# Split weights kept in DRAM after the first block, and chains issued by an estimate of the engines' queues

## The chip, the cores and the metric

The kernel runs on one core of a Trainium2 chip. The time is the device time of one execution in microseconds; the runs of one kernel are summarised by their median.

## What is computed

One layer of a hybrid decoder for 2048 prompt tokens (after 16 learned meta tokens) and 8 sample sequences of 4 tokens, in float32, model width 1024. Four heads of width 128 are retention heads, four are gated delta heads; then come an output projection, a residual LayerNorm, a SwiGLU FFN of width 2816 and another LayerNorm. The core of it, from the reference:

```python
proj = h @ w_in                                     # both head groups, 1024 -> 4104
# retention, chunks of 128 tokens
scores = jnp.einsum('bnhid,bnhjd->bnhij', q, k) * decay
intra = jnp.einsum('bnhij,bnhjd->bnhid', scores, v)
s = chunk_decay * s + jnp.einsum('bhcd,bhce->bhde', kc, vc)
# gated delta rule, chunks of 128 tokens
kk = jnp.einsum('bnhid,bnhjd->bnhij', k, k)
lower = jnp.where(strict, kk * decay, 0.0) * beta[..., :, None]
a_mat = jnp.eye(C, dtype=q.dtype) + lower
sol = lax.linalg.triangular_solve(a_mat, rhs, left_side=True, lower=True, unit_diagonal=True)
u = wv - jnp.einsum('bhcd,bhde->bhce', wk, s)
o = jnp.einsum('bhcd,bhde->bhce', qg, s) + jnp.einsum('bhij,bhje->bhie', at, u)
s = cd * s + jnp.einsum('bhcd,bhce->bhde', kt, u)
# both
mixed = jnp.concatenate([o_r, o_g], -1) @ w_out
hp = layer_norm(ALPHA * hp + mp, ln1_g, ln1_b)
hp = layer_norm(ALPHA * hp + swiglu(hp, w_gate_up, w_down), ln2_g, ln2_b)
```

## The kernel before

**Products in two parts.** A float32 product is made of three matmuls on float32r parts: a value `x` is split into `xh`, its cast, and `xl = x - xh`, and `mm3` (L288) issues `ah bh`, `ah bl` and `al bh`. Weights come from DRAM in float32 and are split on the chip each time they are used: for a piece of 2048 columns, `load_piece` issues two DMAs of 512 KB into the ring `raw` of two buffers (L260, on SyncE's queue, SP), and `split` casts each on ScalarE (ACT, `wh<-raw`, L237) and subtracts on VectorE (DVE, `wl<-raw,wh`, L244). The pair goes to `wring`, which has two buffers: the piece in use and the one after it. `next_piece` hands over the piece whose turn it is and starts the load of the next; with `later=True` the split is put on the list `pend` and issued a few steps later.

**Attention.** The tokens are taken in four blocks of 512 (block 0 holds 48 more rows, meta and sample tokens). In each block the eight heads come in the order "r0 g0 r1 g1 r2 g2 r3 g3" (the last block has another), and each takes two pieces of weights, so the same 16 pieces are loaded and split in each of the four blocks, 64 in all. The projections of a head (`ret_proj`, `gdn_proj`) are long runs of matmuls into the PSUM pool `pj` that depend on little. What follows for a head is a chain of small products, each of which waits for other engines: `ret_chain` for retention; `gdn_chain` with `gdn_group` for the delta rule. The latter makes `LT` from `kT` (L816, L818), then `Z` and `U` on DVE (L827, L828) and the six masks `Lm` on GpSimd (POOL, L830), inverts by block doubling (L834 reads U; L840 and L847 make the products of each level), refines the inverse (the tile `Tf`, L860, L868), runs the recurrence over four chunks (L902 to L922), scales the output on DVE (`V<-V,rqy`, L931) after a reciprocal square root in small DVE steps (`rqa`, `rqt`, `rqy`, L189 to L201), and transposes it (L933).

**The weaving.** The chains are Python generators. While the projections of the next head are issued, `mm3g` yields after every six matmuls or so the time that these take on TensorE (PE), and `advance` subtracts it from a counter for each chain; when the counter is used up, the next step of the chain is issued. What a step puts into its counter is a number of the list `LAT`, which is fixed by hand per kind of step, times 1.0 for retention and 1.8 for the delta rule (`SLACK`). So a step's distance from the one before is a fixed amount of projection work. One retention chain and one delta chain can be under way at a time. Every engine runs its instructions in the order that results from this.

**FFN.** After the attention phase the output projection and the FFN run over two halves of the tokens in the same manner (L1067 on). They are not touched.

Of the kernel before, what the change touches and what calls it, by code (L numbers as in the profile page):

```python
# [148 lines left out]
class _Cut:  # L149
    """Allocates [128, full, ...] tiles and hands out their first n rows of dim 1."""  # L150
# [13 lines left out]

class Builder:
    def __init__(self, tc, I, O):
        self.tc, self.nc, self.I, self.O = tc, tc.nc, I, O
        _, self.off, self.gam, _ = _consts()
        self.es = ExitStack()
# [13 lines left out]
    def rsqrt(self, x, n, rows, pool, scale, eps):  # L183
        """(scale x + eps)^-0.5; x may be a list of equal parts."""
# [19 lines left out]
    def layer_norm(self, src, rows, g, b, pool, fast=False, pinned=False):  # L204
        """LayerNorm of rows in place; src is the row, or its two halves. fast: the vector engine alone."""
# [42 lines left out]
    def load_piece(self, src, ab=False, ring=None, later=False, el="dve"):  # L248
        """2048 (+64) columns of weights as a pair of float32r parts."""
# [7 lines left out]
        lv = l.rearrange("p (a b) -> p a b", a=8)  # L257
        for i in range(2):
# [17 lines left out]
    def mm3g(self, out, lh, ll, rh, rl, kn, per):  # L276
        """As mm3, with a yield of the tensor engine's time after every few k."""
# [6 lines left out]
    def mm3(self, out, lh, ll, rh, rl, kn, first=True, last=True):  # L284
        """out (+)= sum_k l(k)^T r(k), with float32 operands in two float32r parts."""
# [55 lines left out]
    def phase_ln(self, b):  # L341
        """Embedding LayerNorm of the tokens of block b, a tile at a time."""
# [11 lines left out]
    def first_block(self):  # L354
        """As phase_ln and turned for the first block, whose tokens and weights are loaded together."""
# [14 lines left out]
        self.ahead = self.load_piece(*self.todo.pop(0), el="pool")  # L370
# [23 lines left out]
    def phase_t(self, b, tiles, x=None):  # L394
        """Transposes of normalised rows, one tile of tokens at a time."""
# [14 lines left out]
    def next_piece(self):  # L410
        """The weights whose turn it is; the load of those after them starts."""
        w = self.ahead
        while self.pend:
            self.split(*self.pend.pop(0))
        self.age = 0
        self.ahead = self.load_piece(*self.todo.pop(0), later=True) if self.todo else None
        return w

    def ret_proj(self, b, h, gates, out, before=None):
# [39 lines left out]
        if before and b == 0:  # L459
            # the weights come before the tokens: each tile of these meets all of those  # L460
# [20 lines left out]
    def ret_chain(self, b, h, qkvg, mixd):  # L481
        """The retention itself; yields the time until its next products can start."""
# [62 lines left out]

        flip(0)
        yield LAT[0]
        for t in range(n):
            score(t)
            yield LAT[1]  # L550
            if t + 1 < n:
                flip(t + 1)
                yield LAT[2]
            mix(t)
            yield LAT[3]
        rs = self.rsqrt(ss[:, :n], n, 128, self.sm, 4.0 / HD, 4.0 * RMS_EPS)
        yield LAT[4]
        for t, (rows, c0, ch) in enumerate(tiles):
            orow = NS if ch < 0 else 128
            o = oc[t]  # L560
            nc.vector.scalar_tensor_tensor(out=o, in0=o, scalar=rs[:orow, t:t + 1], in1=vg[t][1][:orow], op0=ALU.mult, op1=ALU.mult)
            p = self.prt.tile([128, 128], F32, tag="rt", name="rt")[:, :orow]
# [5 lines left out]
            yield LAT[5]  # L568
# [3 lines left out]
    def state_out(self, kt, u, S0, cd, gam, out):  # L572
        """out_b = decay_b S0_b + kt_b^T u_b for the eight sample sequences."""
# [367 lines left out]
    def attention(self):  # L941
        with ExitStack() as es:
# [21 lines left out]
            while self.active:  # L964
                self.advance(0.3)
# [23 lines left out]
    def finish(self, key):  # L989
        while key in self.active:  # L990
            self.advance(0.3)
# [258 lines left out]
```

## Time and profile before

| | us |
|---|---|
| three runs | 3137.73, 3143.98, 3137.69 |
| median | 3137.73 |
| the profiled execution: its span | 3141.4 |
| PE busy | 2994.8 |
| DVE busy | 1826.4 |
| ACT busy | 967.1 |
| POOL busy | 565.9 |

No time of its own is given for the profiled execution beside its span; the span lies between the shortest and the longest of the three runs, 3.7 above the median. Busy times are sums over the whole span. The attention phase ends at about 1362 us; its blocks begin at about 0, 396, 721 and 1028 us. The trace's rows name a line of the kernel, an engine, an operation and the tiles "out<-in"; PE's times of matmuls are modelled at their ends, so that neighbouring rows overlap.

### The profile page before, as it was taken

The numbers are of one execution on the slowest core, as the hardware profiler recorded it, in microseconds if no ns is written. First come the engines' busy times: TensorE is split into PE (matmuls) and PEld (weight loads), VectorE is DVE, ScalarE is ACT, GpSimd is POOL, SyncE is SP. The second block draws the span as 40 slices with busy tenths as digits, with TensorE's granted clock in tenths as the row PEclk, the third lists the DMA queues.
The fourth block names the chain that finished last, engine by engine and source line by source line (L and its number), as shares of the span: only waits on it lengthen the run. The fifth ranks groups of instructions, "written<-read, shape, count | busy, mean of one in ns | idle before, by whom it ended". The sixth has DMA issues, their size and how long they took to land. (4 is left out here: it accounts for less than half of the span.)

```text
span 3141.4 us, 44842 instructions
## 1 busy us (share of the span) xinstructions
PE 2994.8 (95%) x17858; PEld 2593.6 (83%) x17858; DVE 1826.4 (58%) x4024; ACT 967.1 (31%) x2179; POOL 565.9 (18%) x570
## 2 busy tenths in 40 slices
PE   7999998999999988999999999999999999999997
PEld 6988887888888877878999999998777877878787
DVE  7777777877787777767333333333684343333346
ACT  2434443545544545433111111111233111111111
POOL 1332222221222122202100001110131000001002
PEclk9999998999999999999999999999999999999999
DMA  5222222222222111152111111112242111111111
GB/s 198 85 75 79 95 99 79 88 93 88 78 93 97 59 53 66 48 180 64 54 41 54 41 41 54 41 41 68 71 145 81 41 54 41 54 41 54 40 41 54
DMA packets 91986, 225.28 MB, mean 72 GB/s; under 512 B 10960, under 2 KB 39168, under 8 KB 91776
## 3 DMA queue, kind: packets, MB, share of 16 engines
q1 hardware_dynamic: 91776, 222.41, 21.5%
q8 instruction: 140, 2.29, 0.3%
q14 instruction: 70, 0.57, 0.1%
HBM read 191.87 MB, written 30.51 MB: 71 GB/s over the span
## 5 line engine op out<-in xcount | busy, mean ns | idle before, releaser
L288 PE MATMUL g<-fxT,wh 128*128 128x352 f32 (+2 forms) x3648 | 954.9, 344 | 1.5 <-DVE th L1110 0.6
L288 PEld LDWEIGHTS g<-fxT,wh 128*128 128x128 f32 x3648 | 646.6, 188 | 62.8 <-ACT fxT L237 1.0
L288 PE MATMUL d<-wh,ff 128*128 128x512 f32 (+1 forms) x1912 | 618.3, 397 | 15.8 <-DVE y L1129 6.9
L288 PE MATMUL g<-fxT,wl 128*128 128x352 f32 (+2 forms) x1824 | 626.9, 344 | 0.0
L237 ACT CAST wh<-raw 128x1024 fp32r<-128x1024 f32 x276 | 285.4, 1050 | 637.9 <-PE d L288 407.5
L288 PE MATMUL pj<-wh,xT 128*128 128x256 f32 (+2 forms) x2176 | 458.0, 298 | 14.5 <-DVE rotB L440 8.1
L288 PEld LDWEIGHTS d<-wh,ff 128*128 128x128 f32 (+1 forms) x1912 | 351.1, 184 | 116.5 <-DVE y L1129 16.8
L244 DVE TENSOR_TENSOR wl<-raw,wh 128x1024 fp32r<-128x1024 f32 x274 | 356.5, 1313 | 56.5 <-ACT wh L237 54.8
L288 PE MATMUL pj<-xT,wh 128*128 128x512 f32 (+1 forms) x1280 | 380.3, 379 | 0.8 <-DVE kp L685 0.6
L288 PE MATMUL d<-wl,ff 128*128 128x512 f32 (+1 forms) x956 | 377.9, 395 | 1.7 <-DVE wl L244 1.7
L244 POOL TENSOR_TENSOR ff<-th,ff 128x352 fp32r<-128x352 f32 (+2 forms) x114 | 142.7, 1251 | 1299.7 <-ACT ff L237 1254.8
L288 PEld LDWEIGHTS pj<-wh,xT 128*128 128x128 f32 (+1 forms) x2176 | 357.8, 193 | 20.3 <-issue 8.6
L288 PEld LDWEIGHTS g<-fxT,wl 128*128 128x128 f32 x1824 | 342.4, 188 | 28.8
L1129 DVE TENSOR_TENSOR y<-y,d 128x512 f32<-128x512 f32 (+1 forms) x340 | 231.6, 685 | 187.3 <-PE d L288 187.1
L288 PE MATMUL pj<-wl,xT 128*128 128x256 f32 (+2 forms) x1088 | 319.3, 294 | 0.5 <-POOL wl L244 0.5
L1110 DVE SCALAR_TENSOR_TENSOR th<-th,g 128x352 f32<-128x352 f32 (+2 forms) x114 | 65.2, 572 | 338.3 <-ACT th L1109 338.3
L1111 DVE SCALAR_TENSOR_TENSOR th<-th,g 128x352 f32<-128x352 f32 (+2 forms) x114 | 65.2, 572 | 336.9 <-PE g L288 336.7
L288 PE MATMUL pj<-xT,wl 128*128 128x512 f32 (+1 forms) x640 | 230.1, 360 | 0.0
L288 PEld LDWEIGHTS pj<-xT,wh 128*128 128x128 f32 x1280 | 209.0, 192 | 19.4 <-DVE S L584 3.0
L288 PEld LDWEIGHTS d<-wl,ff 128*128 128x128 f32 (+1 forms) x956 | 175.7, 184 | 44.9 <-DVE wl L244 2.7
L288 PEld LDWEIGHTS pj<-wl,xT 128*128 128x128 f32 (+1 forms) x1088 | 210.4, 193 | 1.1 <-POOL wl L244 0.8
L1109 ACT ACTIVATE th<-g 128x352 f32<-128x352 f32 (+2 forms) x114 | 57.7, 506 | 371.8 <-PE g L288 343.0
(272 smaller groups left out, 3812.6 us busy)
## 6 DMA issues: line engine op xcount, KB each, us to landing
raw<-gu SPq DMA_DIRECT2D x88, 512.0 KB, 3.9
raw<-wret SPq DMA_DIRECT2D x64, 512.0 KB, 4.0
raw<-wgd SPq DMA_DIRECT2D x64, 512.0 KB, 3.9
raw<-dn SPq DMA_DIRECT2D x44, 512.0 KB, 3.9
raw<-wout SPq DMA_DIRECT2D x16, 512.0 KB, 4.2
ff<-mixd SPq DMA_DIRECT2D x16, 512.0 KB, 4.1
y<-xhat SPq DMA_DIRECT2D x16, 512.0 KB, 4.8
out_y<-y SPq DMA_DIRECT2D x16, 512.0 KB, 2.6
```

What stands on the lines that cost most here:

```text
L237: i = nc.scalar.copy(out=h, in_=src)
L244: i = (nc.vector if el == "dve" else nc.gpsimd).tensor_tensor(out=l, in0=src, in1=h.bitcast(F32), op=ALU.subtract)
L288: self.nc.tensor.matmul(out, lhsT=a(k), rhs=b(k), start=first and k == 0 and i == 0, stop=last and k == kn - 1 and i == 2)
L1109: nc.scalar.activation(out=t, in_=ps[0], func=AF.Tanh, scale=0.5)
L1110: nc.vector.scalar_tensor_tensor(out=t, in0=t, scalar=1.0, in1=ps[0], op0=ALU.add, op1=ALU.mult)
L1111: nc.vector.scalar_tensor_tensor(out=t, in0=t, scalar=0.5, in1=ps[1], op0=ALU.mult, op1=ALU.mult)
L1129: nc.vector.tensor_tensor(out=ys, in0=ys, in1=p, op=ALU.add)
```

## The change

**Weights.** Each entry of the list of pieces now has a block and a key. In block 0 a piece is loaded and split as before, and when its turn comes, `next_piece` also writes its two parts to DRAM (the tiles `parts`, 1 MB for `wh` and 1 MB for `wl`). In blocks 1 to 3 `load_piece` reads the two parts back into `wring` with two DMAs and splits nothing.

**Weaving.** `LAT` and `SLACK` are gone. All engine calls go through wrappers that tell a `Meter` of each instruction. It keeps one clock for each engine: an instruction begins when its engine is free and its inputs are made (0.12 us later if another engine made them), and takes a time that is linear in its elements. The PSUM pools are wrapped in `Ring`, which knows when the next buffer comes free. A step of a chain now yields what its next product needs (tiles and pools), and `advance` issues it as soon as the Meter has all of it ready 0.35 us before the end of PE's queue.

```diff
-SLACK = {"r": 1.0, "g": 1.8}
+MARGIN = 0.35
-LAT = [1.0, 0.7, 0.7, 0.7, 2.0, 0.7, 0.5, 1.2, 1.8, 0.9, 1.0, 1.0, 1.7, 1.0, 0.6, 0.5, 0.5]
...
+class Meter:
+    BASE = {"vector": (0.17, 0.00088), "scalar": (0.19, 0.00078), "gpsimd": (0.12, 0.0025)}
+    HOP = 0.12
...
+    def when(self, need):
+        return max([0.0] + [n.next_free() if isinstance(n, Ring) else self.made.get(self.name(n), (0.0, 0))[0] + self.HOP for n in need])
...
+        a, b = self.BASE[engine]
+        if op == "bn_stats":
+            n = 512
+        return a + b * n + (0.2 if kw.get("accum_out") is not None else 0.0)
...
+        t = self.free[engine]
+        for a in ins:
+            end, by = self.made.get(self.name(a), (0.0, engine))
+            t = max(t, end + (0.0 if by == engine else self.HOP))
...
+        end = t + self.took(engine, op, out, kw)
+        self.free[engine] = end
...
+        if kept is not None:
+            for i, t in enumerate((h, l)):
+                nc.sync.dma_start(out=t.bitcast(F32), in_=kept[i, :, :n])
+            return hv, lv
+        if keep is not None:
+            self.keeping[id(hv)] = keep[:, :, :n], h, l
...
+    def load_next(self, **how):
+        b, key, src, ab = self.todo.pop(0)
+        if b == 0:
+            self.parts[key] = self.dr.tile([2, 128, self.wcols], F32, tag=f"parts{key}", name="parts")
+            return self.load_piece(src, ab, keep=self.parts[key], **how)
+        return self.load_piece(src, ab, kept=self.parts[key])
...
     def next_piece(self):
         w = self.ahead
         while self.pend:
             self.split(*self.pend.pop(0))
+        if id(w[0]) in self.keeping:
+            to, *parts = self.keeping.pop(id(w[0]))
+            for i, t in enumerate(parts):
+                self.nc.sync.dma_start(out=to[i], in_=t.bitcast(F32))
         self.age = 0
-        self.ahead = self.load_piece(*self.todo.pop(0), later=True) if self.todo else None
+        self.ahead = self.load_next(later=True) if self.todo else None
...
-        yield LAT[8]
+        yield kT, self.pw
         pl = wide()
...
-        yield LAT[9]
+        yield U, self.pw
         pt = wide()[:R, :m, :R]
...
         for x in range(1, nl):
-            yield LAT[10]
+            yield T, Lm, self.pw
...
+        nc.vector.tensor_tensor(out=O[:orow], in0=O[:orow], in1=rs.unsqueeze(2).broadcast_to([orow, m, 128]), op=ALU.mult)
+        yield O, self.psc
         p = self.psc.tile([128, 4, 128], F32, tag="sc", name="sc")[:, :m, :orow]
-        nc.vector.tensor_tensor(out=O[:orow], in0=O[:orow], in1=rs.unsqueeze(2).broadcast_to([orow, m, 128]), op=ALU.mult)
...
-    def advance(self, us):
+    def advance(self):
         for key in list(self.active):
-            c = self.active[key]
-            c[1] -= us
-            while c[1] <= 0:
-                w = next(c[0], None)
-                if w is None:
+            while key in self.active:
+                c = self.active[key]
+                if self.m.when(c[1]) > self.m.free["tensor"] - MARGIN:
+                    break
+                need = next(c[0], None)
+                if need is None:
                     del self.active[key]
-                    break
-                c[1] += w * SLACK[key]
+                else:
+                    c[1] = need
...
     def finish(self, key):
         while key in self.active:
-            self.advance(0.3)
+            self.advance()
+            if key in self.active:
+                t = min(self.m.when(c[1]) for c in self.active.values()) + MARGIN
+                self.m.free["tensor"] = max(self.m.free["tensor"], t)
```

The two kernels' orders differ at many places. Three are shown. The lists name an instruction's line, operation and tiles; in the changed kernel every instruction has the line of the wrapper, L262, so there the tiles tell them apart.

DVE in block 1, where the third delta head (g2) begins its inverse while the chain of the head before it (tile `V_8073`, in the other kernel `V_7996`) ends. First before, from the last state product on:

```order
L922 SCALAR_TENSOR_TENSOR V_8073<-qs,eg,w 128x128
L244 TENSOR_TENSOR wl<-raw,wh 128x1024
...
L199 TENSOR_TENSOR rqt<-rqy 128x4
L244 TENSOR_TENSOR wl<-raw,wh 128x1024
...
L818 TENSOR_TENSOR LT<-w,mg 128x512
L200 SCALAR_TENSOR_TENSOR rqt<-rqt,rqa 128x4
L827 TENSOR_TENSOR Z<-LT,lvl 128x512
L201 SCALAR_TENSOR_TENSOR rqy<-rqt,rqy 128x4
L439 TENSOR_TENSOR qk<-pj,rott 128x256
L929 TENSOR_TENSOR rqy<-rqy,gsk 128x4
L828 SCALAR_TENSOR_TENSOR U<-Z,ident 128x512
L931 TENSOR_TENSOR V_8073<-V_8073,rqy 128x512
```

The same place after the change:

```order
L262 SCALAR_TENSOR_TENSOR V_7996<-qs,eg,w 128x128
L262 TENSOR_SCALAR rkd<-qk,cb 128x128
L262 TENSOR_TENSOR vb<-w,sv 128x512
...
L262 TENSOR_TENSOR LT<-w,mg 128x512
L262 SCALAR_TENSOR_TENSOR rqy<-rqt,rqy 128x4
L262 TENSOR_TENSOR Z<-LT,lvl 128x512
L262 TENSOR_TENSOR rqt<-rqy 128x4
L262 SCALAR_TENSOR_TENSOR U<-Z,ident 128x512
L262 SCALAR_TENSOR_TENSOR rqt<-rqt,rqa 128x4
L262 TENSOR_TENSOR qk<-pj,rott 128x256
L262 SCALAR_TENSOR_TENSOR rqy<-rqt,rqy 128x4
...
L262 TENSOR_TENSOR V_7996<-V_7996,rqy 128x512
```

The two subtractions behind the last state product are gone, `vb` has moved behind it, and `qk` now comes after U.

PE at the same place, from the product that makes LT's input (`w<-kT`) to the transposes of V (`sc<-ident`); the projection matmuls in between are `pj`, three to a step. Before:

```order
L816 MATMUL w<-kT 128x128 x4
L288 MATMUL pj<-wh,xT 128x256
L288 MATMUL pj<-wl,xT 128x256
L288 MATMUL pj<-wh,xT 128x256 x2
...
L288 MATMUL pj<-wh,xT 128x256 x2
L834 LDWEIGHTS U
L834 MATMUL w<-identh,U 128x128
...
L288 MATMUL pj<-wl,xT 128x256
L288 MATMUL pj<-wh,xT 128x256 x2
L933 MATMUL sc<-ident,V_8073 128x128 x4
```

And after:

```order
L262 MATMUL w<-kT 128x128 x4
L262 MATMUL pj<-wh,xT 128x256 x2
L262 MATMUL pj<-wl,xT 128x256
...
L262 MATMUL pj<-wh,xT 128x256
L262 LDWEIGHTS U
L262 MATMUL w<-identh,U 128x128
...
L262 MATMUL pj<-wh,xT 128x256 x2
L262 MATMUL pj<-wl,xT 128x256
L262 MATMUL pj<-wh,xT 128x256
L262 MATMUL sc<-ident,V_7996 128x128 x4
```

Between `w<-kT` and U stand 25 projection matmuls before and 19 after; between the last state product of the other chain and the transposes of V, 60 before and 37 after.

SP at the start of the kernel, where the second piece of weights is asked for. Before:

```order
L378 DMA xhat<-x 128x512 x2
L260 DMA raw<-wret 128x1024 x2
L524 DMA S_807<-st_ret 128x1024
L378 DMA xhat<-x 128x512 x2
L260 DMA raw<-wgd 128x1024 x2
```

And after:

```order
L262 DMA xhat<-x 128x512 x2
L262 DMA parts<-wh 128x2048
L262 DMA parts<-wl 128x2048
L262 DMA raw<-wret 128x1024 x2
L262 DMA xhat<-x 128x512 x2
L262 DMA S_855<-st_ret 128x1024
L262 DMA parts<-wh 128x2112
L262 DMA parts<-wl 128x2112
L262 DMA raw<-wgd 128x1024 x2
```

The stores of a piece's two parts stand ahead of the loads of the piece after it.

More of the change, by code (lines that the diff above doesn't have):

```diff
@@ new lines, with __init__, next_free, tile @@
+class Ring:
+    of = {}
+    def __init__(self, pool, bufs, meter):
+        self.pool, self.bufs, self.meter = pool, bufs, meter
+        self.busy, self.at = [0.0] * bufs, 0
+    def next_free(self):
+        return self.busy[self.at % self.bufs]
+    def tile(self, *a, **kw):
+        t = self.pool.tile(*a, **kw)
+        i = self.at % self.bufs
+        self.at += 1
+        n = self.meter.name(t)
+        self.meter.used[n] = self.busy[i]
+        Ring.of[n] = self, i
+        return t
+class Timed:
+    def __init__(self, engine, key, meter):
+        self.engine, self.key, self.meter = engine, key, meter
+    def __getattr__(self, op):
+        f = getattr(self.engine, op)
+        def issue(*a, **kw):
+            i = f(*a, **kw)
+            self.meter.note(self.key, op, a, kw)
+            return i
+        return issue
@@ L165, with __init__ @@
+class Engines:
+    def __init__(self, nc, meter):
+        for k in ("tensor", "vector", "scalar", "gpsimd", "sync"):
+            setattr(self, k, Timed(getattr(nc, k), k, meter))
 class Builder:
     def __init__(self, tc, I, O):
-        self.tc, self.nc, self.I, self.O = tc, tc.nc, I, O
+        self.m = Meter()
+        Ring.of = {}
+        self.tc, self.nc, self.I, self.O = tc, Engines(tc.nc, self.m), I, O
         _, self.off, self.gam, _ = _consts()
@@ L246, in split, with load_piece @@
             self.tc.keep_in_program_order(i)
-    def load_piece(self, src, ab=False, ring=None, later=False, el="dve"):
+    def load_piece(self, src, ab=False, ring=None, later=False, el="dve", keep=None, kept=None):
         nc = self.nc
@@ L369, in first_block @@
         g, be = [self.vec_bcast(i, self.ax, "xa") for i in range(2)]
-        self.ahead = self.load_piece(*self.todo.pop(0), el="pool")
+        self.ahead = self.load_next(el="pool")
         load(0, "kT")
@@ L856, in gdn_group @@
         nc.scalar.copy(out=V, in_=U)
-        yield LAT[12]
+        yield T, LT, self.pw
         pe = wide()[:R, :m, :R]
@@ L864, in gdn_group @@
         for it in range(2):
-            yield LAT[13]
+            yield Er, V, self.pw
             pu = wide()[:R, :m, :R]
@@ L950, in attention @@
             self.mp = self.pool("mix", bufs=2, es=es)
-            self.pj = self.pool("p_pj", bufs=2, space=PSUM, es=es)
-            self.pw = self.pool("p_w", bufs=3, space=PSUM, es=es)
-            self.psc = self.pool("p_sc", bufs=1, space=PSUM, es=es)
-            self.prt = self.pool("p_rt", bufs=2, space=PSUM, es=es)
+            self.pj = Ring(self.pool("p_pj", bufs=2, space=PSUM, es=es), 2, self.m)
+            self.pw = Ring(self.pool("p_w", bufs=3, space=PSUM, es=es), 3, self.m)
+            self.psc = Ring(self.pool("p_sc", bufs=1, space=PSUM, es=es), 1, self.m)
+            self.prt = Ring(self.pool("p_rt", bufs=2, space=PSUM, es=es), 2, self.m)
             self.todo, self.pend = [], []
+            self.parts, self.keeping = {}, {}
             for b in range(NBLK):
@@ L963, in attention @@
                 self.attn_block(b)
-            while self.active:
-                self.advance(0.3)
+            for key in ("r", "g"):
+                self.finish(key)
             nc.sync.dma_start(out=self.O["conv"], in_=self.cout)
@@ L1022, in attn_block @@
             for i, us in enumerate(fill):
-                self.advance(us)
+                self.advance()
                 self.age += 1
```

71 lines of the change are left out of this document (56 added, 15 removed).

## The prediction

> **What bounds the kernel now.** I read the page's head and its busy table first, then the windows by stage, then what TensorE (PE) waits for, then what VectorE (DVE) does in a stretch where PE waits.
>
> ```profile
> span 3141.4 us, 44842 instructions
> PE 2994.8 (95%) x17858; PEld 2593.6 (83%) x17858; DVE 1826.4 (58%) x4024; ACT 967.1 (31%) x2179; POOL 565.9 (18%) x570
> ...
> 0.00:40.00 40.00, 20.94 (x117) 18.32 (x118) 32.68 (x96) 9.67 (x15) 7.75 (x15) 0.87 0.73 247
> 40.00:396.00 356.00, 340.99 (x2617) 304.77 (x2615) 264.97 (x707) 154.83 (x466) 99.48 (x118) 0.98 0.28 92
> 396.00:721.00 325.00, 302.42 (x2127) 260.63 (x2127) 250.90 (x640) 154.56 (x412) 77.16 (x87) 0.95 0.27 88
> 721.00:1028.00 307.00, 286.23 (x2073) 252.23 (x2074) 236.85 (x610) 151.05 (x395) 72.46 (x80) 0.97 0.27 88
> 1028.00:1362.00 334.00, 305.07 (x2220) 267.41 (x2219) 251.90 (x605) 157.95 (x412) 75.86 (x90) 0.97 0.18 60
> 1362.00:3141.00 1779.00, 1739.09 (x8711) 1490.26 (x8709) 789.15 (x1372) 339.05 (x480) 233.19 (x180) 0.99 0.18 60
> ```
>
> A window row gives length, busy time of PE, its weight loads, DVE, ACT and POOL, the granted clock, DMA share and GB/s. The rows are the start, attention blocks 0 to 3, and the FFN. PE bounds the span, so time is saved only where PE stands still or runs at a low clock. In blocks 1 to 3, the ones the weight part touches, PE is idle for 22.58 + 20.77 + 28.93 = 72.3 us of 966, and the clock costs another 325 x 0.05 + 307 x 0.03 + 334 x 0.03 = 35.5 us. The FFN loses 40 us of 1779 and its code is unchanged. All that the change could win is therefore some 108 us, 3.4%, and DVE, busy 77% of these blocks on average, is the engine to look at.
>
> ```profile
> PE w L834 <- DVE U L828: 22.8, 12, 3.5
> PE sc L933 <- DVE V L931: 15.4, 11, 3.1
> PE pj L288 <- DVE rotB L440: 7.7, 3, 3.1
> PE sc L910 <- DVE r L905: 5.8, 7, 1.3
> PE pt L406 <- DVE rqy L201: 4.6, 2, 2.3
> ...
> L244 DVE TENSOR_TENSOR wl<-raw,wh 128x1024 fp32r<-128x1024 f32 x96 | 119.8, 1254 | 10.0 <-ACT wh L237 9.6
> ```
>
> These are PE's waits in 396:1362 (total, times, longest) and the largest DVE group there. Nearly every wait ends with DVE. Two of them, U at the start of the delta rule's inverse and V, the scaled output of the previous head's chain, make 38.2 us. One stretch shows how:
>
> ```profile
> 632.00:668.00 36.00, 30.43 (x213) 27.00 (x212) 34.55 (x88) 13.91 (x38) 14.24 (x13) 0.97 0.37 121
> 668.00:715.00 47.00, 47.00 (x339) 41.17 (x337) 29.23 (x61) 26.35 (x64) 4.88 (x10) 0.95 0.28 84
> ...
> 658.25 1.21 DVE L244 TENSOR_TENSOR wl<-raw,wh 128x1024 fp32r<-128x1024 f32 x1
> ...
> 661.49 0.69 DVE L818 TENSOR_TENSOR LT<-w,mg 128x512 f32<-128x512 f32 x1
> ...
> 662.82 1.11 DVE L201 SCALAR_TENSOR_TENSOR rqy<-rqt,rqy 128x4 f32<-128x4 f32 x1
> ...
> 664.97 0.68 DVE L828 SCALAR_TENSOR_TENSOR U<-Z,ident 128x512 f16<-128x512 f16 x1
> 665.57 1.64 DVE L931 TENSOR_TENSOR V<-V,rqy 128x512 f32<-128x512 f32 x1
> ...
> 665.71 0.61 PE L834 MATMUL w<-identh,U 128*128 128x128 f16 x4 [3.48 <-DVE U L828]
> ```
>
> For 36 us DVE is 96% busy and PE is not, and then PE runs without a gap while DVE has slack. So PE does not wait for one slow operation: DVE has fallen behind, and U and V come last in its queue. A single DVE item taken out anywhere in that stretch brings U nearer by its own length. The stretch is the third delta head of block 1, whose rows of the order stand above.
>
> **The weight part.** It takes 96 subtractions of 1.254 us off DVE in blocks 1 to 3 (the row above) and as many casts off ACT, which binds nothing. The 120 us are not the gain: only what lies in a stretch where DVE is behind counts. To size it I went, for each of the twelve delta heads of these blocks, from the last product of the previous chain's inverse (the tile Tf) to this head's U and to the V that follows, and summed along both orders the DVE work and the PE work that lie between, each kind of instruction at its mean duration in the trace. DVE work minus PE work is what PE must wait if DVE never rests.
>
> Before: 6.9 us in each of four heads, 5.9 in two, 3.2, 2.5 and 2.3 in three, 0.2 or less in three. Sum 48. The head quoted is one with 6.9 (38.2 of DVE against 31.3 of PE). Its measured gaps in that stretch are 36.00 - 30.43 = 5.6 us, so the method reads a little high. With the change: 5.6 in four heads, 2.9 in two, none in the others. Sum 28. Four subtractions stood in most of these windows and none does now.
>
> **The weave part** is in that same sum, since the orders of the changed kernel hold both. It works in the opposite direction at these two places. Chains are let go sooner, and the cover becomes thinner: the PE work between the product that makes LT's input and the one that reads U falls from 3.74 to 2.37 us (median of the sixteen heads), and between the last state product and V's transposes from 8.27 to 6.21. In the rows shown, 25 projection matmuls become 19 ahead of U and 60 become 37 ahead of V, each of 0.117 us:
>
> ```profile
> 660.78 0.40 PE L288 MATMUL pj<-wh,xT 128*128 128x256 f32 x2
> 661.01 0.28 PE L288 MATMUL pj<-wl,xT 128*128 128x256 f32 x1
> 661.13 0.39 PE L288 MATMUL pj<-wh,xT 128*128 128x256 f32 x2
> ```
>
> (three matmuls from 660.78 to 661.13). DVE from LT to U shrinks there too: one 128x256 product and one rsqrt step of the previous head now come after U, not before. For this head alone, counted only from the last state product, the two nearly cancel; over windows from vb to U and V the sum goes down by only 5 us, and by U and V taken apart (35.3 to 25.3 and 36.1 to 32.2) by 14. So the change of idle time lies between -5 and, at the other end, -35 (a subtraction saves its full 1.254 us: four of them are 5.0 of a deficit of 6.9, and 48 x 5.0 / 6.9 = 35). I take **-20**, the long window's difference, because the stretch above shows DVE behind from its start, which only that window counts.
>
> What follows the clock: 35.5 us of clock loss came with 72.3 of idle, 0.49 per us. The place where it comes from is behind the gap:
>
> ```profile
> 665.00:672.00 7.00, 6.08 (x31) 0.54 0.11 40
> 685.00:700.00 15.00, 15.00 (x106) 1.00 0.25 71
> ...
> 819.17 1.11 PE L933 MATMUL sc<-ident,V 128*128 128x128 f32 x4 [2.75 <-DVE V L931]
> ...
> 819.00:822.50 3.50, 3.09 (x15) 0.51 0.02 5
> ```
>
> After the 3.48 us gap PE is granted 0.54 of its clock, later all of it; the same follows a gap of 2.75. So -20 of idle gives **-10** more (bounds -2.5 to -17). [...]
>
> **The kept weights' traffic.** Blocks 1 to 3 read two parts in place of one, 2.1 MB a piece. The start's window moves 247 GB/s at a share of 0.73, that is 338 at full share, so a piece needs 6.2 us and with the landing of a lone transfer
>
> ```profile
> raw<-wret SPq DMA_DIRECT2D x64, 512.0 KB, 4.0
> mixd<-Uf SPq DMA_DIRECT2D x16, 256.0 KB, 2.0
> ...
> raw<-wret SPq DMA_DIRECT2D x2, 512.0 KB, 7.2
> ```
>
> some 8 to 10 us; the upper end, four transfers of 512 KB one behind the other at 4.0, is 16. In the changed order the PE work from the release of a buffer to the first use of its next content is 13.2 us at least and 16 in the median, and PE's waits lengthen it. The stores of mixed outputs that stand ahead on SP take at most 1.6 us of that. I cost it at **0**, hidden behind projection matmuls; at 16 us it would show in a few pieces by up to 3 us each.
>
> **The start.** The changed order on SP puts the stores of the first piece's two parts, 2 MB, ahead of the loads of the second piece. Now:
>
> ```profile
> 26.59 1.18 SPq L260 DMA_DIRECT2D raw<-wret  x2
> 33.47 1.04 ACT L237 CAST wh<-raw 128x1024 fp32r<-128x1024 f32 x1 [3.30 <-DMA raw<-wret]
> 34.56 0.46 PE L288 MATMUL pj<-wh,xT 128*48 128x264 f32 x1 [1.42 <-ACT wh L237]
> 35.80 2.84 SPq L260 DMA_DIRECT2D raw<-wgd  x2
> 55.14 2.00 ACT L237 CAST wh<-raw 128x1024 fp32r<-128x1024 f32 x2 [2.15 <-PE pj L288]
> ```
>
> PE already waits for that load, which takes 7.2 us here (the last row of the fence before, from 22:40). With 2 MB ahead at 247 to 338 GB/s it comes 6.2 to 8.5 us later, and nothing but PE's few remaining transposes covers it. Cost **+7**, between 0 (if other transfers then waiting give way) and 8.5. The next piece is asked for at 35.80 and cast at 55.14, so the stores ahead of it, and of the later ones, are covered. Block 0 keeps all its splits; its weave changes, and I put that at 0, between -3 and +3, since PE is idle for only 15.0 us of its 356, against 72.3 of 966 in the other blocks.
>
> **Sum.** -20 - 10 + 0 + 7 + 0 = -23 us on a profiled execution of 3141.4, hence 3118; that execution lies within the three runs (3137.69, 3137.73, 3143.98) but 3.7 above their median, so in terms of the median 3137.7 - 23 = **3115**. Its own range by the bounds of the idle term, with the clock that goes with it, is 3093 (-35 - 17 + 7) to 3132.
>
> **Rivals.**
> Nothing gained: the thinner cover eats what the subtractions free. That is the -5 of the short windows: -5 - 2.5 + 7 = 0, 3137, with a spread of 3130 to 3143. For it: those windows count exactly the PE work that was taken away. Against it: they leave out that DVE is behind when they begin. Also here: kept weights without an effect.
>
> Slower: the estimate lets chains go too early. It takes a vector operation of 512 elements as 0.17 + 0.00088 x 512 = 0.62 us and has no term for another engine's interference. The trace:
>
> ```profile
> L828 DVE SCALAR_TENSOR_TENSOR U<-Z,ident x14: 678/884/1657, 428.2 to 1302.2; 128x512 f16<-128x512 f16 x13, 48x48 f16<-48x48 f16 x1
> 662.26 5.97 POOL L830 TENSOR_TENSOR Lm<-LT,lvl 128x512 f16<-128x512 f32 x4 [1.17 <-DVE rqt L200]
> ```
>
> U takes from 678 to 1657 ns, 884 in the median, and a 128x4 operation 1.11 us in place of 0.15 while POOL makes Lm from 662.26 on. If DVE's real work between LT, U and V does not shrink, the cover taken away is paid in full: the larger loss, 8.27 - 6.21 = 2.06 us, in each of 12 heads is 25 us of idle, with 12 of clock and 7 at the start +44, **3182**. It decides from the point at which cover falls faster than DVE work; in the orders cover falls by 1.37 us at U and DVE from LT to U by about 0.6 in blocks 1 to 3, so U alone is on the wrong side, and only the removed subtractions outweigh it. [...]
>
> Larger gain: once a sixth of DVE's work in these blocks is gone (119.8 of 739.7), its backlog does not build up, and all waits for DVE go, about 55 of the 72 us. -55 - 26 + 7 = -74, **3064**. Against it: four heads keep a deficit of 5.6 us in the orders.
>
> Kept weights late: if a piece takes 4 x 7.2 = 29 us as at the start, against 13 to 16 of lead, 48 pieces at 13 us give 620 us, **3760**; the low DMA share of blocks 1 to 3 (0.18 to 0.27 with a load of half the size) speaks against it.
>
> **How the numbers follow.** Forecast 0.45, nothing gained 0.22, larger gain 0.13, slower by thin cover 0.15, late weights 0.05. About 0.2% (6 us) is what a measurement can tell from no change, so faster means below 3131.5. Faster: 0.44 + 0.13 + 0.05 of the second case = 0.62; same: 0.01 + 0.13 = 0.14; slower: 0.04 + 0.15 + 0.05 = 0.24. The range 3062 to 3145 holds the forecast, the nothing-gained case and the larger gain, 0.8 together.
>
> **What would show it.** No wl in 396:1362 and DVE some 115 us less busy there; waits for U and V down from 38 to about 22 us, the four heads with 3.5 us gaps still among them; granted clock of the three blocks up by a hundredth; a wait of 8 us at about 35 us from the start, ended by the cast of raw; no wait of PE for wh or wl loaded from parts. I am wrong if waits for U or V grow, if a new wait shows inside the inverse (its first step now waits for all of Lm, which POOL makes), or if PE waits for kept weights.

## The result, and the profile after

The changed kernel takes 3175.35 us (median of four, 3172.59 to 3179.78) against 3137.71 before: a ratio of 1.0117, 95% interval 1.0103 to 1.0132. It is slower by 1.2%, where 0.7% faster was forecast. The profiled executions spanned 3171.0 and 3141.4 us; the span of before lies 3.7 us above its median time, that of the changed kernel 4.4 below, so the profiles show 30 of the 38 us.

The windows of the changed kernel (length, then PE, weight loads, DVE, ACT, POOL, clock, DMA share, GB/s), cut where PE begins each block's transposes:

```profile
span 3171.0 us, 44659 instructions
PE 3002.9 (95%) x17858; PEld 2608.8 (82%) x17858; DVE 1734.1 (55%) x3922; ACT 885.1 (28%) x2083; POOL 545.6 (17%) x570
...
0.00:412.00 412.00, 366.93 (x2718) 326.06 (x2719) 295.21 (x795) 161.57 (x475) 96.55 (x133) 0.94 0.55 192
412.00:749.00 337.00, 308.76 (x2146) 269.55 (x2144) 217.81 (x608) 128.91 (x386) 72.36 (x87) 0.93 0.35 129
749.00:1058.00 309.00, 284.48 (x2073) 254.00 (x2073) 209.19 (x578) 124.28 (x365) 70.42 (x80) 0.97 0.39 142
1058.00:1395.00 337.00, 305.86 (x2230) 270.58 (x2228) 224.19 (x576) 134.24 (x386) 74.17 (x90) 0.96 0.29 107
1395.00:3171.00 1776.00, 1736.84 (x8696) 1488.61 (x8696) 787.71 (x1369) 336.12 (x475) 232.07 (x180) 0.99 0.18 60
```

The same cuts in the kernel before:

```profile
0.00:392.00 392.00, 359.01 (x2710) 320.65 (x2711) 293.65 (x784) 162.57 (x477) 107.23 (x133) 0.97 0.32 106
392.00:721.00 329.00, 305.34 (x2151) 263.07 (x2149) 254.90 (x658) 156.49 (x416) 77.16 (x87) 0.95 0.28 90
721.00:1028.00 307.00, 286.23 (x2073) 252.23 (x2074) 236.85 (x610) 151.05 (x395) 72.46 (x80) 0.97 0.27 88
1028.00:1365.00 337.00, 307.49 (x2233) 269.06 (x2231) 253.87 (x609) 160.95 (x418) 75.86 (x90) 0.97 0.18 60
```

Block 0 is 20 us longer, block 1 is 8, blocks 2 and 3 are 2 and 0; the FFN is the same. DVE is 94 us less busy in blocks 1 to 3 (651.2 against 745.6; some 115 was expected), and yet PE is not less idle there: 83.9 us against 73.9. In block 0 it is idle for 45.1 us against 33.0, and the clock is 0.94 against 0.97. Of the 30 us, 22 are idle time of PE and 8 are busy time, all 8 in block 0.

PE's waits in blocks 1 to 3 of the changed kernel, then in block 0 behind the start (total, times, longest):

```profile
PE sc L262 <- DVE V L262: 34.6, 12, 5.1
PE w L262 <- DVE U L262: 19.5, 10, 2.5
PE pj L262 <- DVE xT L262: 6.7, 3, 3.1
...
PE w L262 <- DVE U L262: 7.4, 4, 2.5
PE sc L262 <- DVE V L262: 5.6, 3, 3.3
```

The two waits that were to shrink from 38.2 to about 22 us have grown to 54.1: V's from 15.4 to 34.6, while U's fell from 22.8 to 19.5. Block 0 has 13.0 us of the two, where before there were about 2. One head shows what holds V up, the third delta head of block 1, the one that the prediction quoted:

```profile
684.72 0.69 DVE L262 TENSOR_TENSOR LT<-w,mg 128x512 f32<-128x512 f32 x1
685.33 0.15 DVE L262 SCALAR_TENSOR_TENSOR rqy<-rqt,rqy 128x4 f32<-128x4 f32 x1
685.49 8.21 POOL L262 TENSOR_TENSOR Lm<-LT,lvl 128x512 f16<-128x512 f32 x6 [2.18 <-DVE rqy L262]
686.05 1.11 DVE L262 TENSOR_TENSOR rqt<-rqy 128x4 f32<-128x4 f32 x1
687.09 0.68 DVE L262 SCALAR_TENSOR_TENSOR U<-Z,ident 128x512 f16<-128x512 f16 x1
687.69 1.12 DVE L262 SCALAR_TENSOR_TENSOR rqt<-rqt,rqa 128x4 f32<-128x4 f32 x1
687.82 0.40 PE L262 MATMUL w<-identh,U 128*128 128x128 f16 x4 [2.29 <-DVE U L262]
691.08 1.60 DVE L262 TENSOR_TENSOR V<-V,rqy 128x512 f32<-128x512 f32 x1
692.74 1.12 PE L262 MATMUL sc<-ident,V 128*128 128x128 f32 x4 [2.15 <-DVE V L262]
```

No subtraction is left in this stretch. DVE's work, beside U and what leads to it and the products of the next retention head (left out here), is the last steps of the old chain's reciprocal square root, 128x4 elements each. Ahead of POOL's masks such a step takes 0.15 us; beside them 0.86 to 1.12. V itself takes 1.60 us, where its median is 0.70. From the start of LT to the end of V pass 8.0 us. POOL begins the masks 0.8 us after the start of LT and is still at them when V ends, 8.2 us in all.

### The profile page after: what moved, and what is told of

Read it like the earlier page. It is cut to its first block, busy times and chain, and to the rows that moved or that the text cites. A ratio compares the mean times of both kernels' runs of the same rounds, so it can differ in the third digit from the quotient of the medians.

```text
span 3171.0 us, 44659 instructions
## 1 busy us (share of the span) xinstructions
PE 3002.9 (95%) x17858; PEld 2608.8 (82%) x17858; DVE 1734.1 (55%) x3922; ACT 885.1 (28%) x2083; POOL 545.6 (17%) x570
## 3 DMA queue, kind: packets, MB, share of 16 engines
q8 instruction: 140, 2.29, 0.3%
## 5 line engine op out<-in xcount | busy, mean ns | idle before, releaser
L262 PE MATMUL g<-fxT,wh 128*128 128x352 f32 (+2 forms) x3648 | 955.0, 345 | 1.2 <-DVE th L262 0.6
L262 PEld LDWEIGHTS g<-fxT,wh 128*128 128x128 f32 x3648 | 646.4, 188 | 62.7 <-DVE th L262 1.2
L262 PE MATMUL d<-wh,ff 128*128 128x512 f32 (+1 forms) x1912 | 618.1, 397 | 15.4 <-DVE y L262 9.1
L262 PE MATMUL g<-fxT,wl 128*128 128x352 f32 (+2 forms) x1824 | 626.7, 344 | 0.0
L262 DVE SCALAR_TENSOR_TENSOR th<-th,g 128x352 f32<-128x352 f32 (+2 forms) x228 | 130.4, 572 | 673.8 <-ACT th L262 337.0
L262 PE MATMUL pj<-wh,xT 128*128 128x256 f32 (+2 forms) x2176 | 469.9, 303 | 12.7 <-DVE xT L262 6.7
L262 PEld LDWEIGHTS d<-wh,ff 128*128 128x128 f32 (+1 forms) x1912 | 351.0, 184 | 116.2 <-DVE y L262 17.8
L262 PEld LDWEIGHTS pj<-wh,xT 128*128 128x128 f32 (+1 forms) x2176 | 365.0, 197 | 17.8 <-DVE xT L262 7.5
L262 PE MATMUL d<-wl,ff 128*128 128x512 f32 (+1 forms) x956 | 377.9, 395 | 1.7 <-DVE wl L262 1.7
L262 PE MATMUL pj<-xT,wh 128*128 128x512 f32 (+1 forms) x1280 | 367.8, 371 | 0.6 <-ACT cpre L262 0.4
L262 PEld LDWEIGHTS g<-fxT,wl 128*128 128x128 f32 x1824 | 342.4, 188 | 28.8
L262 POOL TENSOR_TENSOR ff<-th,ff 128x352 fp32r<-128x352 f32 (+2 forms) x114 | 141.5, 1242 | 1300.1 <-ACT ff L262 1255.3
L262 ACT CAST wh<-raw 128x1024 fp32r<-128x1024 f32 x180 | 184.1, 1048 | 623.7 <-PE d L262 407.6
L262 DVE TENSOR_TENSOR y<-y,d 128x512 f32<-128x512 f32 (+1 forms) x340 | 231.5, 685 | 187.4 <-PE d L262 187.3
L262 PE MATMUL pj<-wl,xT 128*128 128x256 f32 (+3 forms) x1088 | 322.7, 297 | 0.5 <-POOL wl L262 0.5
L262 DVE TENSOR_TENSOR wl<-raw,wh 128x1024 fp32r<-128x1024 f32 x178 | 239.0, 1359 | 53.1 <-ACT wh L262 50.7
L262 PEld LDWEIGHTS pj<-xT,wh 128*128 128x128 f32 x1280 | 214.7, 191 | 23.5 <-ACT cpre L262 0.8
L262 PE MATMUL pj<-xT,wl 128*128 128x512 f32 (+1 forms) x640 | 228.1, 356 | 0.0
L262 PEld LDWEIGHTS pj<-wl,xT 128*128 128x128 f32 (+1 forms) x1088 | 213.7, 196 | 1.4 <-POOL wl L262 0.8
L262 PEld LDWEIGHTS d<-wl,ff 128*128 128x128 f32 (+1 forms) x956 | 175.8, 184 | 44.6 <-DVE wl L262 2.3
L262 ACT ACTIVATE th<-g 128x352 f32<-128x352 f32 (+2 forms) x114 | 57.6, 505 | 370.2 <-PE g L262 342.9
L262 ACT CAST ff<-th 128x352 fp32r<-128x352 f32 (+2 forms) x114 | 60.0, 526 | 282.4 <-DVE th L262 282.4
```

Source lines behind the costliest of these rows:

```text
L262: i = f(*a, **kw)
```

## The experiments

Times are medians, ratios those to the kernel before on the same chip, with their 95% intervals. "U+V" is PE's waits for these two over the attention phase behind the start, "idle" span less PE's busy time, both of the profiled execution.

| kernel | us | ratio | U+V | idle | PE busy |
|---|---|---|---|---|---|
| before | 3137.7 | 1 | 40 | 147 | 2995 |
| changed | 3175.4 | 1.0117 [1.0103, 1.0132] | 67 | 168 | 3003 |
| weights alone | 3124.0 | 0.9943 [0.9923, 0.9962] | 32 | 134 | 2984 |
| weave alone | 3193.1 | 1.0158 [1.0134, 1.0183] | 48 | 165 | 3029 |
| changed, MARGIN 1.5 | 3200.9 | 1.0188 [1.0167, 1.0209] | 64 | 166 | 3033 |
| changed, MARGIN -0.8 | 3150.9 | 1.0030 [1.0018, 1.0042] | 23 | 140 | 3014 |
| changed, stores behind | 3177.6 | 1.0113 [1.0092, 1.0134] | 64 | 168 | 3009 |
| old numbers in block 0 | 3147.1 | 1.0016 [1.0004, 1.0027] | 53 | 153 | 2994 |
| old numbers in blocks 1-3 | 3146.4 | 1.0013 [1.0000, 1.0025] | 42 | 142 | 3006 |
| no Lm in the needs | 3166.3 | 1.0078 [1.0059, 1.0097] | 72 | 160 | 3004 |
| old in block 0, MARGIN -0.8 | 3139.0 | 0.9999 [0.9990, 1.0009] | 22 | 138 | 2998 |
| old in block 0, MARGIN -2 | 3152.4 | 1.0042 [1.0026, 1.0057] | 18 | 143 | 3008 |
| retention by old numbers | 3160.0 | 1.0066 [1.0051, 1.0081] | 66 | 164 | 2996 |
| delta rule by old numbers | 3138.8 | 1.0002 [0.9990, 1.0015] | 38 | 142 | 2994 |
| changed, one mask | 3092.1 | 0.9843 [0.9828, 0.9857] | 24 | 113 | 2980 |
| weights alone, one mask | 3104.1 | 0.9889 [0.9867, 0.9910] | 23 | 120 | 2984 |
| changed, chain start held | 3140.7 | 0.9997 [0.9986, 1.0008] | 42 | 138 | 3006 |
| changed, masks on DVE | 3127.6 | 0.9961 [0.9946, 0.9976] | 26 | 139 | 2987 |
| changed, Meter knows POOL | 3174.2 | 1.0107 [1.0092, 1.0122] | 63 | 160 | 3012 |
| weights alone, masks on DVE | 3097.2 | 0.9856 [0.9835, 0.9876] | 16 | 118 | 2977 |

### The two parts apart

Weights alone: the kernel before, with `load_next`, the stores and the ready-split loads of the diff, and LAT and SLACK as they were. Weave alone: the changed kernel with

```diff
-            self.parts[key] = self.dr.tile([2, 128, self.wcols], F32, tag=f"parts{key}", name="parts")
-            return self.load_piece(src, ab, keep=self.parts[key], **how)
-        return self.load_piece(src, ab, kept=self.parts[key])
+            return self.load_piece(src, ab, **how)
+        return self.load_piece(src, ab, **how)
```

> The kernel before with the kept weights alone; the chains are woven by the old list of numbers. In its order the PE work ahead of V's transposes (from the last state product) falls from 8.27 to 5.66 us in the median and that ahead of U from 3.74 to 3.08, although the list is the old one. Theory A (the new weave thins the cover, the kept weights by themselves gain): faster, 3137.7 - 25 to 40, about 3105. Theory B (cover shrinks wherever subtractions leave DVE, because the order is made by durations that are too short, so a wait is the part that these miss and the removal of splits does not shorten it): 3140 to 3165, with waits for V in blocks 0 to 3 of more than the 17 us of before. Theory C (traffic of the parts): 3150 or more, with waits for wh, wl or for the other loads.

> The changed kernel with every piece loaded and split in each block as before; the chains are woven by the Meter. Its order has 3.99 us of PE work ahead of U and 8.57 ahead of V's transposes in the median, as much as before or more. Theory A (the new weave is at fault): slower than the changed kernel's 3175 by the subtractions that are back, about 3195. Theory B (the removed subtractions thin the cover): 3125 to 3145, waits for U and V together no more than the 40 us of before.

The weights gain 0.6% and the weave costs 1.6%; together that is 1.0%, near the 1.2% of the change. Theory B fell on both sides: the weights alone do gain, though less than A had it, and the weave alone is slow although its order has more PE work ahead of V than before. So cover as counted in the order is not what decides.

In the weights alone PE's idle time in blocks 1 to 3 falls from 73.9 to 54.9 us and DVE is 115 us less busy there, both as the prediction had it for the whole change (this profile is of the fastest of the kernel's four runs, 4 us below their median). In the head that the prediction quoted, PE waited 3.48 us for U and 0.21 for V before; now it is none for U and 1.85 for V:

```profile
657.23 0.69 DVE L948 TENSOR_TENSOR V<-V,rqy 128x512 f32<-128x512 f32 x1
657.84 0.69 DVE L835 TENSOR_TENSOR LT<-w,mg 128x512 f32<-128x512 f32 x1
...
657.98 0.66 PE L950 MATMUL sc<-ident,V 128*128 128x128 f32 x4 [1.85 <-DVE V L948]
658.60 7.68 POOL L847 TENSOR_TENSOR Lm<-LT,lvl 128x512 f16<-128x512 f32 x6 [1.69 <-DVE LT L835]
...
662.71 0.40 PE L851 MATMUL w<-identh,U 128*128 128x128 f16 x4
```

Here V is done before POOL begins the masks. With the weave on top, U+V grows by 35 us (32 to 67), PE's idle time by 34 and its busy time by 19, so these two waits grow by as much as all idle time does. The weave alone differs: against the kernel before, U+V grows by 8 us only, idle by 18 and busy time by 35. Most of that loss is not in these waits, and its cause is not shown.

### Too early or too late

```diff
-MARGIN = 0.35
+MARGIN = 1.5
```

> The changed kernel with MARGIN 1.5 in place of 0.35: a step is let go when its inputs are ready 1.5 us ahead of the end of PE's queue. Theory A (steps are let go too early): each step has 1.15 us more cover, the 29 waits for U and V of 67 us lose about 33 us and half as much of the clock, 3125 to 3140. Theory B (the yields do not decide the cover at U and V): 3165 to 3180, since its order has only 0.35 us more ahead of U and nothing more ahead of V in the median.

> The changed kernel with MARGIN -0.8: a step is let go 1.15 us earlier than by 0.35. Theory A (steps come too early, thin cover): slower than 3175, 3195 or more. Theory D (steps come too late: the Meter holds a chain back until all inputs are made, the head's projections run out, and what is left of the chain runs bare, without projections between its steps, with waits and at half clock): its order has 10 us less bare chain work in block 0 (55 us against 65 in the changed kernel, 51 before), so block 0 loses about half of its 33 us, 3155 to 3165.

The direction is the opposite of theory A's: letting steps go later costs another 0.7%, letting them go earlier gains 0.9%. With -0.8 the stretch from the first step of V's reciprocal square root to the end of V takes 3.7 us in the median of the heads, against 10.1 in the changed kernel, and U+V falls to 23 us. Summed over all heads, POOL makes masks beside these stretches for 10 us, against 98 in the changed kernel, 47 before and 20 in the weights alone. But PE's busy time is the second highest of the kernels here with kept weights: other waits (14.1 us for kp) and slower matmuls may take back part of the gain, which was not followed further.

### The stores at the start

The two stores of a piece are issued after the loads of the next one in `next_piece`.

```diff
-        (the stores)
         self.age = 0
         self.ahead = self.load_next(later=True) if self.todo else None
+        (the stores)
```

> The changed kernel with the two stores of a piece issued behind the loads of the next piece, not ahead of them. If the stores cost what the start's wait for the cast shows (3.44 us against 1.42, 4.5 us later on PE), 3170 to 3172; if the stores hold up more of block 0, 3160; if they cost nothing, 3175.

The wait for the cast falls from 3.44 to 1.57 us, and nothing is gained by the end. The weights alone, too, are 6 us late at the 81st projection matmul and level with before at the 891st of 5184. I read this as slack of the pieces after it that the start uses up; no run tests it.

### Where, and which chains

A hybrid gives each step both its old number and its needs; a chain goes by one or the other. It was not run with the old numbers everywhere.

```diff
-        yield kT, self.pw
+        yield LAT[8], (kT, self.pw)
...
-                if self.m.when(c[1]) > self.m.free["tensor"] - MARGIN:
+                if c[2] > 0 if c[3] else self.m.when(c[1]) > self.m.free["tensor"] - MARGIN:
```

> The changed kernel with the old numbers (LAT, SLACK) deciding in block 0 and the Meter in blocks 1 to 3, kept weights in both. By the times at which the projections get through in the runs so far, the changed kernel loses 33 us up to the first projections of block 1 and then gains 3 on the kernel before. If that loss is the weave's in block 0: 3175 - 28 to 33, 3142 to 3148. If the stores of the parts have a share in it: 3155 or more.

> The changed kernel with the Meter in block 0 and the old numbers in blocks 1 to 3, kept weights in both. If the weave costs what the weights give in blocks 1 to 3 (the weights alone gain 24 us there, the changed kernel 3): 3175 - 21, about 3154. If the loss is the start's and block 0's alone: 3172.

> The changed kernel with the old numbers in block 0 and the Meter with MARGIN -0.8 in blocks 1 to 3, kept weights in both. Theory D (in blocks 1 to 3 the Meter lets steps go too late): block 0 as with the old numbers (394 us in that run), blocks 1 to 3 as with MARGIN -0.8 (953 us), FFN 1776: 3123 on the profile, 3125. If the gain of MARGIN -0.8 in blocks 1 to 3 was only what it had lost in block 0: 3147.

> As the run with the old numbers in block 0 and MARGIN -0.8 in blocks 1 to 3, but with MARGIN -2.0. Theory D: as fast or faster, 3120 to 3126. Theory A (below some point the cover is too thin): 3135 or more, with longer waits in the recurrence and the inverse.

> The changed kernel with the old numbers for retention in all blocks and the Meter for the delta chains. If what costs is chain work left over without projections beside it: its order has less of it than the kernel before (43 and 60 us in block 0 and in the others, against 51 and 72 before and 65 and 90 in the changed kernel), 3120 to 3135. If the delta chains' own covers cost (U, V): 3165 or more.

> The changed kernel with the old numbers for the delta chains in all blocks and the Meter for retention. If what costs is chain work left over without projections: its order has 63 us of it in block 0 and 72 in the others, so block 0 loses as in the changed kernel, 3145 to 3155. If the delta chains' own covers cost: as the weights alone, 3125.

The old numbers give back 1.0% in block 0 and 1.0% in blocks 1 to 3. My account by the times at which projections get through had three fifths of it in block 0; the first run came out as it said, the second 8 us faster. The two gains together, 2.0%, are a little more than the weave costs (1.7%); that chain work left over crosses the cut and is paid in the next block is a reading, not tested. The delta chains cost 1.0066 - 0.9943 = 1.2%, retention 1.0002 - 0.9943 = 0.6%, together about what the weave adds to the weights (1.0117 - 0.9943 = 1.7%). Counting chain work without projections beside it ranked the last two runs the wrong way round, so that theory fell as well. In blocks 1 to 3, -0.8 gains 0.2% on 0.35, between the two cases named for it, and -2 loses 0.4% on that: none of the margins tried brings the Meter to the old numbers (0.9943).

### What holds U and V up

In the first run the first doubling step no longer waits in the Meter for all masks. In the two with one mask POOL makes one of the six masks and all levels use it; this leaves out five sixths of the mask work and changes the inverse.

```diff
-            yield T, Lm, self.pw
+            yield T, self.pw
```

```diff
-        for x in range(1, nl):
+        for x in range(1, 2):
             nc.gpsimd.tensor_tensor(out=Lm[:, x - 1], in0=LT, in1=lvl(x), op=ALU.mult)
...
-                nc.tensor.matmul(py[:, i, :], lhsT=Lm[:, x - 1, i, :], rhs=T[:, i, :], start=True, stop=True)
+                nc.tensor.matmul(py[:, i, :], lhsT=Lm[:, 0, i, :], rhs=T[:, i, :], start=True, stop=True)
```

> The changed kernel without Lm in the needs of the doubling steps, so that the first of them does not wait in the Meter for all six masks that POOL makes. In its order the PE work in bare stretches of block 0 is 53 us, against 65. Theory D (late chains): 3155 to 3165. Theory A (thin cover): 3175 or slower, with waits of the first doubling product for Lm.

> The changed kernel with one of the six masks Lm: POOL makes the mask of the second level alone and all doubling steps read it, so that the inverse is not the reference's. Its PE order is that of the run without Lm in the needs (1.0078 of the kernel before). Theory L (the small DVE steps ahead of V, and U, are held up while POOL makes Lm beside them): waits for U and V, 67 us in the changed kernel, fall below 35, and the time to 3125 to 3140. Rival (the waits come from the length of these dependent steps and the thin cover alone): as without Lm in the needs, 3155 to 3167.

> The kernel with the weights part alone, with one of the six masks Lm, so that the inverse is not the reference's; the PE order is the same. Theory L: the U and V waits of that kernel, 32 us, fall to 15 or less, 3100 to 3110. Rival: 3118 to 3124, as with all masks.

Taking Lm out of the needs gains 0.4%, and U+V does not shrink (72 us). The second run has the same order on PE as the first, but for one projection matmul at four places, and 74 us lie between them, where 26 to 41 were expected. U+V falls by 48 us, PE's idle time by 47 and its busy time by 24, at a granted clock of 0.985 against 0.973. The waits without Lm in the needs, all masks made, and then with one mask:

```profile
PE sc L262 <- DVE V L262: 39.8, 12, 5.0
PE w L262 <- DVE U L262: 32.6, 18, 3.1
```

```profile
PE sc L262 <- DVE V L262: 5.9, 7, 1.8
PE w L262 <- DVE U L262: 18.2, 12, 2.6
```

V's waits fall to 5.9 us. On the old numbers the same edit is worth 0.5%, and U+V falls to 23 us where 15 or less was expected. So POOL's masks slow DVE in both kernels (V's longest duration is 1.6 us in each; it is 0.69 with one mask, in the order without Lm in the needs, and 0.69 in the weights alone once DVE makes the masks), and the weave puts more of DVE's short dependent steps beside them. The traces have a measure of it: what DVE's instructions of the attention phase take above the shortest tenth of their own kind (operation, output and shape) sums to 123 us before, 100 in the weights alone, 128 in the changed kernel and 147 in the weave alone; with one mask it is 75. DVE's busy time says the same: the same 3922 instructions take 1709 us in the weights alone, 1734 in the changed kernel and 1675 in that with one mask.

Two edits test that from the other side: the masks made by DVE, and the start of a delta chain (the steps v, kp, kT, U) held to the old numbers' distance as well as to the Meter.

```diff
-            nc.gpsimd.tensor_tensor(out=Lm[:, x - 1], in0=LT, in1=lvl(x), op=ALU.mult)
+            nc.vector.tensor_tensor(out=Lm[:, x - 1], in0=LT, in1=lvl(x), op=ALU.mult)
```

> The changed kernel with all six masks Lm made by DVE in place of POOL. Theory L: no POOL work stands beside U and V any more; DVE has some 80 x 0.69 = 55 us more to do in blocks 1 to 3, after U. Waits for U and V below 35 us and 3100 to 3125, between the run with one mask (3092) and that of the weights alone (3124). If the removal of mask work as such made the run with one mask fast: 3140 to 3165, since DVE does more.

> The weights part alone, old numbers, with all six masks Lm made by DVE. Theory L: its 32 us of waits for U and V fall to 20 or less, 3105 to 3118 against 3124. If DVE's added work costs as much: 3120 to 3130.

> The changed kernel, in which the four steps from the start of a delta chain to U (v, kp, kT, U) must wait both for the Meter and for the old numbers' distance; all other steps go by the Meter. Its order has 2.96 us ahead of U (2.37 in the changed kernel), 5.08 ahead of V (6.21). If the loss comes from a chain's start running into the end of the chain before it: waits for U and V about 35 to 45 us, 3145 to 3158. If it comes from chains being late: as slow or slower, 3170 to 3190, since every delta chain gets longer.

All work is kept here, and DVE has 108 masks more in the two runs that move them; in the changed kernel its busy time is nevertheless 1719 us, less than 1734. The same head with the masks on DVE, in the changed kernel:

```profile
668.54 0.69 DVE L262 TENSOR_TENSOR LT<-w,mg 128x512 f32<-128x512 f32 x1
...
671.22 0.16 DVE L262 TENSOR_TENSOR rqt<-rqy 128x4 f32<-128x4 f32 x1
671.29 0.69 DVE L262 TENSOR_TENSOR Lm<-LT,lvl 128x512 f16<-128x512 f32 x1
671.89 0.16 DVE L262 SCALAR_TENSOR_TENSOR rqt<-rqt,rqa 128x4 f32<-128x4 f32 x1
...
673.92 0.69 DVE L262 TENSOR_TENSOR V<-V,rqy 128x512 f32<-128x512 f32 x1
```

From LT to the end of V it is 6.1 us in place of 8.0, with five of the masks in between: in this head a mask of 0.69 us on DVE delays V less than the same mask on POOL. The weights alone with masks on DVE are the fastest kernel of the study that does all the work, 1.4% faster than before and faster than expected. In the changed kernel the edit is worth 48 us, a little less than expected, and holding the chain's start, which leaves 19 of the 98 us of masks beside the old chain's end, 35, a little more. The masks' place is not all of the weave's cost, though: with the masks on DVE the weave still costs 1.0% (0.9961 against 0.9856), and masks then stand ahead of V on DVE itself, as in this head; with one mask, in the order without Lm in the needs, it costs nothing (0.9843 against 0.9889).

### The Meter told of it

```diff
+        if engine == "vector" and t < self.free["gpsimd"]:
+            end += min(0.9, self.free["gpsimd"] - t)
```

> The changed kernel, whose Meter adds to a DVE instruction that begins while POOL is busy up to 0.9 us. Theory L with the Meter's blindness as the step that failed: steps keep more distance, 3145 to 3160. If only the collision itself matters and no distance helps: 3168 to 3178.

No effect: U+V stays at 63 us. The Meter's missing term is not by itself what fails. My reading, not tested: knowing that V comes late, it can only let V's product go later; it does not keep the next chain's masks from starting beside V's steps.

## Why the prediction was wrong

- **The step that failed is "The weave part is in that same sum".** It gave the weave no term of its own: the two orders, counted at mean durations, made -20 us of idle time for both parts together, with 28 us of waits left. Measured, idle time in blocks 1 to 3 is 10 us more with both parts and 19 us less with the weights alone; U and V are waited for 54.1 us, and the weave alone costs 1.6%. Work counted at mean durations cannot show what becomes slow because of what it now lies beside. The weave puts the end of one delta chain beside the masks of the next (98 us, against 20 in the weights alone), and with one mask 48 of the 72 us of these waits are gone.
- **The reading of the bound** held for U, on the order from which it was read. In the weights alone the four waits of 3.5 us for U are 0 to 0.6 us. But others for U grew, so that those of blocks 1 to 3 went from 22.8 to 13.2 us in all, and those for V in the same four heads went from between 0.2 and 0.8 us to 1.9, which the reading did not have. And the step from DVE's busy time to a backlog took all of it for work. With no subtraction left, that head's waits in the changed kernel are still 2.29 and 2.15 us, and part of the busy time is instructions held beside POOL's masks (up to 1.12 us for a 128x4 step there, 0.15 ahead of them). The row of 1.11 us for 128x4 elements stood in the prediction, but only in a rival.
- **The weights part** was right in sign. Alone it is worth 18 us (24 between the two profiles), and U+V falls from 40 to 32 us. That this is near the sum's 23 to 30 is partly luck, since the sum was counted on the orders of the whole change.
- **The clock** followed the idle time, in the other direction: it is 0.94 against 0.97 in block 0 and 0.93 against 0.95 in block 1. PE's busy time grew by 8 us with 22 of idle, 0.37 per us, where 0.49 was used.
- **Block 0 at 0, between -3 and +3**, was wrong: the block is 20 us longer, of which the start's delay is 4.5 at the most. The low idle time of before was taken for a sign that nothing could be lost there.
- **The start** was mis-sized: 2.0 us more wait and 4.5 us later (39.06 in the row below, 34.56 before), not 7, and in the weights alone it is recovered within block 0.

```profile
39.06 0.67 PE L262 MATMUL pj<-wh,xT 128*48 128x264 f32 x2 [3.44 <-ACT wh L262]
```

- **Kept weights' traffic at 0** held: no wait of PE for wh or wl from `parts` is among its listed waits.
- **The rival "slower"** came true in size (3182 named, 3175 measured) and in its cause by half: interference from Lm, as it said. The size is luck in part: it put 37 us into blocks 1 to 3 and 7 into the start, and the profiles show 10 in those blocks and 20 in block 0. Its measure, lost cover, was refuted: a larger MARGIN made it worse. Its chance of 0.15 was too low: the trace already had the row. In the head shown above the 128x4 rows of 0.86 to 1.12 us lie beside the masks (1.16 us each in the median of all), against 0.15 ahead of them. Not every DVE operation beside masks is held, though: U took 0.68 us in the same place. By what means POOL's work holds up DVE's, no run here shows.
- **A slip in the sum:** by its own bounds the range of the forecast ends at 3137 (-5 - 2.5 + 7), not at 3132.

What stays open: why retention by the Meter costs 0.6%, why the weave alone raises PE's busy time by 35 us, what of the weave's cost remains with the masks on DVE, and what raises PE's busy time when steps come earlier.

## What to carry to other kernels

Before taking work off a busy engine, separate its instructions' least durations from the excess: here a 128x4 operation of 1.1 us, where its neighbours took 0.15, was not load but was held up beside POOL's masks. When a schedule is made by estimated queues, look at what it puts side by side, the end of one chain and the start of the next above all, and test each part of a change alone.

## What was not expected of the hardware

In the weights alone and in the changed kernel a mask made by POOL (1.16 us in the median of the latter) cost PE more than the same mask on the engine that PE waits for, where it took 0.69: moving 108 of them to the busier DVE gained 0.9% on the old numbers (0.9943 to 0.9856) and 1.6% on the Meter (1.0117 to 0.9961). U's longest duration fell with it:

```profile
L262 DVE SCALAR_TENSOR_TENSOR U<-Z,ident x20: 192/679/1646, 120.1 to 1334.6; 128x512 f16<-128x512 f16 x16, 48x48 f16<-48x48 f16 x4
...
L262 POOL TENSOR_TENSOR Lm<-LT,lvl x108: 266/1161/2132, 119.4 to 1339.7; 128x512 f16<-128x512 f32 x96, 48x48 f16<-48x48 f32 x12
```

in the changed kernel, and with the masks on DVE:

```profile
L262 DVE SCALAR_TENSOR_TENSOR U<-Z,ident x20: 190/684/690, 122.4 to 1295.0; 128x512 f16<-128x512 f16 x16, 48x48 f16<-48x48 f16 x4
```

Also, in the changed kernel PE was granted half its clock (0.50 from 198.5 to 202.5 us) where the end of a delta chain runs without projections, and no gap of more than 1.3 us stands in the 10 us ahead of it; in the kernel before, clocks of 0.54 and 0.51 came after gaps of 3.48 and 2.75 us. In the changed kernel PE was busy for 2.58 and 2.07 us of the two stretches of 3.40 just before, with short products, some of 32 or 48 rows:

```profile
190.10:193.50 3.40, 2.58 (x16) 1.00 0.03 5
193.50:196.90 3.40, 2.07 (x10) 1.00 0.22 62
...
196.50 3.37 PE L262 MATMUL pj<-ub,kt 32*128 32x512 f32 x4 [1.00 <-DVE ub L262]
...
195.00:207.00 12.00, 11.00 (x52) 0.72 0.32 105
```
